# Index cast of the expert choice from ScalarE to VectorE, and another spread of the compression steps, their weight loads and the subtractions beside them

## The chip, the cores and the metric

The kernel runs on one core of a Trainium2 chip. The metric is the device time of one execution in microseconds (us); lower is better. PE is TensorE, DVE is VectorE, ACT is ScalarE, POOL is GpSimd, SP is SyncE. ACT, DVE and POOL each work through one queue in order, so an instruction that waits holds up all that stands behind it on its engine.

## The reference

One decoder layer for 512 tokens of width 1024: a gated linear recurrence (RG-LRU) beside a sparse attention (NSA), merged, then a product-key expert layer (PEER) and a per-layer embedding. Cut to what the change touches:

```python
z_rx, z_rg, z_q, z_kv, z_ng, z_m = split(rmsnorm(h) @ w_in)

# RG-LRU: r, ig are sigmoids of block-diagonal products of xf
log_a = -LRU_C * r * softplus(-lam)
a = exp(log_a)
u = sqrt(-expm1(2.0 * log_a)) * (ig * xf)
hs = scan(a, u)                       # h[t] = a[t] h[t-1] + u[t]
y_a = (hs * gelu(z_rg)) @ w_a

# NSA: 31 blocks of 32 keys (and of 32 values) are compressed by a small MLP
blk = t[:, idx] + pe
hid = gelu(flat(blk) @ w1 + b1)       # w1: 4096 x 256, for keys and for values
kc, vc = hid_k @ w2_k + b2_k, hid_v @ w2_v + b2_v

# PEER: 16 of 16384 experts for each of 8 heads and each token
best, ci = top_k(cand, 16)            # cand: sums of two sorted lists of 16
e_idx = i1[ci // 16] * 128 + i2[ci % 16]
g = softmax(best)
out = sum(gelu(x . u[e_idx]) * g * v[e_idx])
```

## The kernel before, in words

**Products in three parts.** Every float32 product is three PE passes: an operand is cast to fp32r ("hi") and the rest is src - hi ("lo"), and hi·hi, hi·lo and lo·hi are added in PSUM (`mm3`, L131 to L134). `split` (L124 to L129) makes the two: L126 is a cast on ACT, L128 a cast on DVE or POOL, L129 the subtraction (on DVE unless an engine is passed).

**The projections.** The input projection goes through w_in in chunks of 128 columns; a chunk is 24 matmuls of 128x512 (8 k-slices, three passes). `plan` sets the order in which the chunks are loaded by SP, and `look` splits a chunk (`w8_split`, L174) up to three chunks ahead of its product, into a pool of three `w8` buffers. For the chunks of this stage the cast is on DVE (`hi_eng`) and the subtraction on POOL.

**The stage the change spreads anew** (some 90 to 190 us in the profile). After eight `rx` chunks and two `kc` chunks (the compressed keys' input) come ten chunks in the order `seq`: rg0 to rg3, vc0, vc1, rg4 to rg7. "rg" is the gate z_rg (its evacuation is a gelu on ACT, L514), "vc" is the input of the compressed values (its evacuation writes `blk`: L433 adds, L128 casts on DVE, L129 subtracts on POOL). Between k-slices of these chunks, at the places that the table `CSTEP` gives, one step of the generator `compress()` is put on PE: one of 16 "hid" steps for the keys or 16 for the values (four matmuls of 128x256, L478), a copy `hs` (L481), or the transpose `hidT` with its gelu (L485, L488). A hid step needs 256 KB of w1: SP loads it (L446) into one of four buffers (`w1buf`, `w1half`), ACT casts it, DVE subtracts (`w1_split`), two steps ahead of PE (`LAW` is 3).

**The list `side`.** Work of the recurrence is put between chunks by `run_side`: `lru_b(c)` (ACT: tanh and exp; DVE: a square, L406, and L407), `lru_sqrt` (ACT, two of 128x2048, L412), `rot_c` and `rot_d` (sines, L274 to L279), `lru_c(c)` (DVE: a product, L417, and the scan, L418). Sine, square root, exp and gelu need different ACT tables, so ACT loads a table when it goes from one to the other.

**What follows.** `vs` and `vw` are the attention's values: 64 matmuls of 128x256 with the hi weights (L575, L576), then 32 with the lo weights. Then attention, output products, and the expert layer.

**The expert layer.** `choose(i)` is a generator for each of four groups of 128 tokens. It searches on DVE (sorted lists of 8 by MAX8, FIND_INDEX8, MATCH_REPLACE8), casts the found index `bi` to f16 (`ci`, L1161, ACT), folds it into two table positions (L1170 to L1188) and makes the one-hot tables `oh` (L1243, L1244) that the products G (L1220) read. Each `yield n` gives PE about n ns of fill: steps of the product `xu` of 128 rows of the table u with all tokens, whose weights are cast on ACT (`uh`, L1066) and subtracted on DVE (`ul`, L1071), with an evacuation on ACT (`ac`, L1081). Before the cast of `ci`, `choose` puts the next group's scores on PE and four copies of them (L981) on ACT. The gathers of the chosen rows are indirect DMAs from POOL, consumed on DVE (L1272, L1278).

The lines that set the places of the stage before:

```python
seq = [("rg", i) for i in range(4)] + [("vc", 0), ("vc", 1)] + [("rg", i) for i in range(4, 8)]
CSTEP = [(), (), (1, 2, 4, 5, 7), (0, 1, 3, 4, 6, 7), (0, 2, 3, 5, 6, 7), (), (), (1, 2, 4, 5, 7), (0, 1, 3, 4, 6, 7), (0, 2, 3, 5, 6, 7)]
```

Of the kernel before, what the change touches and what calls it, by code (L numbers as in the profile page):

```python
# [94 lines left out]
def tile_hybrid(ctx, tc, a, out, dbg=None):  # L95
# [61 lines left out]
    plan += [chunk("rg", i) for i in range(4)] + [chunk("vc", 0), chunk("vc", 1)]  # L157
    plan += [chunk("rg", i) for i in range(4, 8)]
# [40 lines left out]
    def gemm(jobs, nside=1, nxt=()):  # L199

        keys = [j[:2] for j in jobs] + list(nxt)
        for n, (name, i, mh, ml, evac) in enumerate(jobs):
            look(keys[n:n + 3])
            w = ready.pop((name, i))
            o = bank("z_" + name)
            if key0 == keys[n]:
# [10 lines left out]
            run_side(nside)  # L217
# [84 lines left out]
    y8, e8, s8, q8, t8, ncoef, pcoef = (const.tile([128, 8], F32, name=n)  # L302
                                        for n in ("y8", "e8", "s8", "q8", "t8", "ncoef", "pcoef"))
# [137 lines left out]
    w1n = [0, 0]  # L441

    def w1_load(upto):
        while w1n[0] < min(upto, 32):
            j, l0 = divmod(w1n[0], 16)
            SP.dma_start(w1buf[w1n[0] % 4], a["cmp_w1"][j][:, 2 * l0:2 * l0 + 2].rearrange("p l c -> p (l c)"))  # L446
            w1n[0] += 1

    def w1_split(upto):
        while w1n[1] < min(upto, 32):  # L450
            n = w1n[1]
            split(w1hl[:, n % 4, 0], w1hl[:, n % 4, 1], w1buf[n % 4])
# [6 lines left out]
    gemm([("kc", i, nhi, nlo, ev_kv(0)) for i in range(2)], nside=3, nxt=[("rg", 0), ("rg", 1)])  # L459
# [75 lines left out]
    seq = [("rg", i) for i in range(4)] + [("vc", 0), ("vc", 1)] + [("rg", i) for i in range(4, 8)]  # L535
    CSTEP = [(), (), (1, 2, 4, 5, 7), (0, 1, 3, 4, 6, 7), (0, 2, 3, 5, 6, 7), (), (), (1, 2, 4, 5, 7), (0, 1, 3, 4, 6, 7), (0, 2, 3, 5, 6, 7)]
    for n, key in enumerate(seq):
# [3 lines left out]
        for k in range(KD):  # L541
# [3 lines left out]
            if n > 3 and k in (1, 5):  # L545
                run_side(1)
# [5 lines left out]
        run_side(3 if n == 0 else 0)  # L552
    for _ in comp:
        pass
    hi_eng[0] = None
    hghi = at.tile([128, 8, S], F32R, name="hghi", tag="big0")
    hglo = at.tile([128, 8, S], F32R, name="hglo", tag="big1")
# [574 lines left out]
    def choose(i, order):  # L1132
# [28 lines left out]
        A.copy(ci.rearrange("p (k h) -> p h k", h=NH), bi)  # L1161
# [13 lines left out]
        yield 4250  # L1175
# [400 lines left out]
```

## Time and profile before

| what | value |
|---|---|
| three runs | 1902.70, 1902.98, 1907.99 us, median 1902.98 |
| the profiled execution, its own time | 1904.83 us |
| its span (first to last instruction) | 1902.8 us |
| mean granted TensorE clock | 0.989 of 2.4 GHz |
| busy: PE, DVE, ACT, POOL | 96%, 74%, 44%, 35% of the span |
| chain that ended last, by engine | PE 70%, DVE 17%, issue 3%, ACT 3%, DMA 1% |

PE is busy for 96% of the span, so the time is PE's work and its idle stretches; those are found by asking which instructions PE waited for, and in which window. "Busy" of an engine is the time in its instructions; a table by windows shows it for one stretch, with the share of full clock that TensorE was granted ("PEclk"). A row of a timeline gives start, duration, engine, line, operation, tile out<-in, partitions x elements, and how many alike follow each other; in brackets the idle time before it and what ended that.

### The profile page before, as it was taken

To read this page: it belongs to the slowest core of one execution; us is meant where nothing else is said; L and a number is where in the kernel's file an instruction comes from. 1 tells how busy PE (TensorE), PEld (TensorE's weight loads), DVE (VectorE), ACT (ScalarE), POOL (GpSimd) and SP (SyncE) were. 2 spreads that over 40 slices of the span, in tenths; PEclk is the share of its full clock that TensorE was granted. 3 is DMA by queue.
4 is the path that set the end of the run, shared out by engine and by line. 5 is a ranking of instruction groups with operands and counts; after the bars stand their busy time and mean duration, and the time that the engine had idled before them with its cause. 6 is when DMAs were issued, how large, how long until landed. Compare 5 with 4: busy or idle time off the path is not lost.

```text
span 1902.8 us, 26515 instructions
## 1 busy us (share of the span) xinstructions
PE 1820.9 (96%) x9817; PEld 1592.5 (84%) x9817; DVE 1410.3 (74%) x2642; ACT 834.6 (44%) x1268; POOL 664.6 (35%) x406
## 2 busy tenths in 40 slices
PE   7988999999999999899999999999999999999997
PEld 6767888777779879899899898888888899999986
DVE  6887516666633368998998977888878788888864
ACT  4463323444521434574674663333333333333353
POOL 3443444322135325334335321222222255556400
PEclk9989999999999999999999999999999999999999
DMA  4253232211024525696796998999999899999941
GB/s 170 101 169 114 78 104 74 67 56 45 23 67 166 194 93 193 234 360 245 252 343 240 339 354 311 360 352 354 353 344 353 306 337 338 343 344 344 359 182 45
DMA packets 181858, 433.29 MB, mean 228 GB/s; under 512 B 14560, under 2 KB 88032, under 8 KB 181728
## 3 DMA queue, kind: packets, MB, share of 16 engines
q1 hardware_dynamic: 124272, 250.35, 37.9%
q0 software_dynamic: 37728, 137.38, 19.9%
q10 hardware_dynamic: 19728, 43.86, 6.1%
q8 instruction: 77, 1.26, 0.3%
q14 instruction: 53, 0.43, 0.1%
HBM read 382.25 MB, written 49.28 MB: 227 GB/s over the span
## 4 chain that ended last, share of the span: by engine, by line
PE 70%; DVE 17%; issue 3%; ACT 3%; DMA 1%; POOL 0%; DVEq 0%; ACTq 0%; POOLq 0%
PE va L134 9%; PE va L132 9%; PE va L133 9%; PE xu L134 6%; PE xu L132 6%; PE xu L133 6%; DVE ul L1071 2%; DVE oh L1243 2%; DVE gr L1272 2%; DVE acc L1278 1%; PE G L1220 1%; PE hid L478 1%; PE z_w_a L132 1%; PE z_w_b L133 1%; PE z_w_a L133 1%
## 5 line engine op out<-in xcount | busy, mean ns | idle before, releaser
L134 PE MATMUL xu<-x2hi,ul 128*128 128x384 f32 x1008 | 339.5, 337 | 10.4 <-DVE ul L1071 10.4
L132 PE MATMUL xu<-x2hi,uh 128*128 128x384 f32 x1008 | 343.7, 341 | 2.7 <-ACT ac L1081 2.0
L133 PE MATMUL xu<-x2lo,uh 128*128 128x384 f32 x1008 | 338.3, 336 | 0.0
L132 PE MATMUL va<-v,A 128*128 128x512 f32 x768 | 299.1, 389 | 1.5 <-ACT A L126 1.5
L134 PE MATMUL va<-v,A 128*128 128x512 f32 x768 | 299.2, 390 | 0.0
L133 PE MATMUL va<-v,A 128*128 128x512 f32 x768 | 298.8, 389 | 0.0
L1257 POOL DMA_INDIRECT gr<-in_peer_u,eidx x128 | 167.3, 1307 | 333.1 <-DVE gr L1272 260.4
L1257 POOL DMA_INDIRECT gr<-in_peer_v,eidx x128 | 185.5, 1449 | 278.0 <-DVE acc L1278 218.2
L126 ACT CAST v<-vring 128x1024 fp32r<-128x1024 f32 x128 | 134.7, 1053 | 256.4 <-issue 146.5
L129 DVE TENSOR_TENSOR v<-vring,v 128x1024 fp32r<-128x1024 f32 x128 | 156.5, 1223 | 63.1 <-ACT v L126 63.0
L134 PEld LDWEIGHTS xu<-x2hi,ul 128*128 128x128 f32 x1008 | 190.2, 189 | 12.9 <-DVE ul L1071 12.9
L132 PEld LDWEIGHTS xu<-x2hi,uh 128*128 128x128 f32 x1008 | 190.6, 189 | 5.1 <-ACT ac L1081 2.3
L133 PEld LDWEIGHTS xu<-x2lo,uh 128*128 128x128 f32 x1008 | 190.4, 189 | 1.9
L132 PEld LDWEIGHTS va<-v,A 128*128 128x128 f32 x768 | 144.1, 188 | 30.2 <-ACT A L126 1.8
L134 PEld LDWEIGHTS va<-v,A 128*128 128x128 f32 x768 | 144.1, 188 | 30.2 <-DVE A L129 0.3
L133 PEld LDWEIGHTS va<-v,A 128*128 128x128 f32 x768 | 144.2, 188 | 28.3
L1278 DVE SCALAR_TENSOR_TENSOR acc<-gr,dots,acc 128x1024 f32<-128x1024 f32 x128 | 163.9, 1281 | 2.6 <-DMA gr<-in_peer_v,eidx 1.0
L1272 DVE SCALAR_TENSOR_TENSOR gr<-gr,x2g 128x1024 f32<-128x1024 f32 x128 | 156.8, 1244 | 5.5 <-DMA gr<-in_peer_u,eidx 5.5
L1066 ACT CAST uh<-ur 128x1024 fp32r<-128x1024 f32 x126 | 132.5, 1053 | 61.1 <-ACT ac L1081 31.1
L1081 ACT ACTIVATE ac<-xu 128x384 f32<-128x384 f32 x128 | 64.3, 502 | 181.6 <-PE xu L134 166.8
L1071 DVE TENSOR_TENSOR ul<-ur,uh 128x1024 fp32r<-128x1024 f32 x101 | 124.8, 1242 | 11.4 <-ACT uh L1066 6.0
L1223 ACT ACTIVATE gst<-G 128x512 f32<-128x512 f32 x96 | 100.3, 1155 | 19.8 <-PE G L1220 19.6
(446 smaller groups left out, 3644.6 us busy)
## 6 DMA issues: line engine op xcount, KB each, us to landing
vring<-in_peer_v SPq DMA_DIRECT2D x128, 512.0 KB
ur<-in_peer_uT SPq DMA_DIRECT2D x126, 512.0 KB
gdram<-gst ACTq DMA_DIRECT2D x12, 2048.0 KB
gt<-gdram SPq DMA_DIRECT2D x32, 768.0 KB
xdram<-ac ACTq DMA_DIRECT2D x88, 192.0 KB
vring<-xdram SPq DMA_DIRECT2D x88, 192.0 KB
raw_m<-in_w_in SPq DMA_DIRECT2D x16, 512.0 KB
raw_rx<-in_w_in SPq DMA_DIRECT2D x8, 512.0 KB
```

The lines of the kernel that those rows point to most:

```text
L126: A.copy(hi, src)
L129: (eng or V).tensor_tensor(lo, src, f(hi), op=OP.subtract)
L132: T.matmul(o, sh, mh, start=start, stop=False)
L133: T.matmul(o, sh, ml, start=False, stop=False)
L134: T.matmul(o, sl, mh, start=False, stop=stop)
L1066: A.copy(us[e][0], urs[e])
L1071: (G if search[0] else V).tensor_tensor(us[e][1], urs.pop(e), f(us[e][0]), op=OP.subtract)
L1081: A.activation(ac, o[:, :ND], AF.Gelu_apprx_tanh)
L1223: A.activation(gst[:, :, c:c + 4].rearrange("p a t -> p t a"), o.rearrange("p (t a) -> p t a", t=4), AF.Copy, scale=1.0 / GSC)
L1257: G.indirect_dma_start(out=r, out_offset=None, in_=tab, in_offset=bass.IndirectOffsetOnAxis(ap=eidx[:, j:j + 1], axis=0))
L1272: V.scalar_tensor_tensor(r, r, 1.0, x2g, op0=OP.mult, op1=OP.mult, accum_out=dots[:, j:j + 1])
L1278: V.scalar_tensor_tensor(acc, r, dots[:, j:j + 1], acc, op0=OP.mult, op1=OP.add)
```

## The change

Two parts of the program are touched.

**The choice.** The cast of `bi` to `ci` is put on DVE instead of ACT, in all four groups, and one `yield` has 4700 for 4250, so a little more fill goes ahead of the next step.

**The stage of gates and compression.** The chunk order is rg0 to rg5, vc0, vc1, rg6, rg7. The subtractions of these chunks' weights, of `blk` and of the vs weights are on DVE instead of POOL. The loads of w1 are issued from POOL instead of SP; a step's subtraction comes one step after its cast, and the load that fills its buffer again after that. The square of `lru_b` is a second exp on ACT (coefficient doubled) instead of a DVE product. The hid steps are fewer in each chunk (4, 4, 4, 5, then 4 and 6), and seven of them go into the vs hi product. Square roots, sines and scans go into vc0, vc1, rg6 and rg7 (table `SIDE`), and two `lru_b` each into rg3 and rg4. The split of the small weight `wg`, and `lru_d`, come after the vs hi product.

```diff
-    plan += [chunk("rg", i) for i in range(4)] + [chunk("vc", 0), chunk("vc", 1)]
-    plan += [chunk("rg", i) for i in range(4, 8)]
+    plan += [chunk("rg", i) for i in range(6)] + [chunk("vc", 0), chunk("vc", 1)]
+    plan += [chunk("rg", i) for i in range(6, 8)]
...
-        split(w[:, 0], w[:, 1], r, G, hi_eng[0])
+        split(w[:, 0], w[:, 1], r, lo_eng[0], hi_eng[0])
...
             if c < 8:
+                a2s[c] = t2("a2")
                 A.activation(tt[:, c], rr[:, c], AF.Tanh, scale=pcoef[:, c:c + 1])
+                A.activation(a2s[c], rr[:, c], AF.Exp, scale=n2coef[:, c:c + 1])
                 A.activation(rr[:, c], rr[:, c], AF.Exp, scale=ncoef[:, c:c + 1])
             if c > 0:
-                a2 = t2("a2")
-                V.tensor_tensor(a2, rr[:, c - 1], rr[:, c - 1], op=OP.mult)
-                V.scalar_tensor_tensor(tt[:, c - 1], a2, 1.0, tt[:, c - 1], op0=OP.add, op1=OP.mult)
+                V.scalar_tensor_tensor(tt[:, c - 1], a2s.pop(c - 1), 1.0, tt[:, c - 1], op0=OP.add, op1=OP.mult)
...
-                split(blk[j][:, ab, :, 0, c], blk[j][:, ab, :, 1, c], t, G, V)
+                split(blk[j][:, ab, :, 0, c], blk[j][:, ab, :, 1, c], t, V, V)
...
-            SP.dma_start(w1buf[w1n[0] % 4], a["cmp_w1"][j][:, 2 * l0:2 * l0 + 2].rearrange("p l c -> p (l c)"))
+            G.dma_start(w1buf[w1n[0] % 4], a["cmp_w1"][j][:, 2 * l0:2 * l0 + 2].rearrange("p l c -> p (l c)"))
...
-            split(w1hl[:, n % 4, 0], w1hl[:, n % 4, 1], w1buf[n % 4])
+            A.copy(w1hl[:, n % 4, 0], w1buf[n % 4])
             w1n[1] += 1
+            w1_lo(n)
+        if upto >= 32:
+            w1_lo(32)
+
+    def w1_lo(upto):
+        while w1n[2] < upto:
+            n = w1n[2]
+            V.tensor_tensor(w1hl[:, n % 4, 1], w1buf[n % 4], f(w1hl[:, n % 4, 0]), op=OP.subtract)
+            w1n[2] += 1
             w1_load(n + 5)
...
-    gemm([("kc", i, nhi, nlo, ev_kv(0)) for i in range(2)], nside=3, nxt=[("rg", 0), ("rg", 1)])
+    lo_eng[0] = V
+    gemm([("kc", i, nhi, nlo, ev_kv(0)) for i in range(2)], nside=(2, 1), nxt=[("rg", 0), ("rg", 1)])
...
-    CSTEP = [(), (), (1, 2, 4, 5, 7), (0, 1, 3, 4, 6, 7), (0, 2, 3, 5, 6, 7), (), (), (1, 2, 4, 5, 7), (0, 1, 3, 4, 6, 7), (0, 2, 3, 5, 6, 7)]
+    seq = [("rg", i) for i in range(6)] + [("vc", 0), ("vc", 1)] + [("rg", i) for i in range(6, 8)]
+    CSTEP = [(), (), (1, 3, 5, 7), (1, 3, 5, 7), (1, 3, 5, 7), (0, 2, 3, 5, 7), (), (), (4, 5, 6, 7), (0, 1, 3, 4, 6, 7)]
+    SIDE = [(5,), (), (), (0, 0), (0, 0), (1,), (0, 0, 4), (0, 3, 6), (1, 2, 5), (1, 4, 6)]
...
+                if br == 0 and k % 4 == 3:
+                    next(comp, None)
...
-        A.copy(ci.rearrange("p (k h) -> p h k", h=NH), bi)
+        V.tensor_copy(ci.rearrange("p (k h) -> p h k", h=NH), bi)
...
-        yield 4250
+        yield 4700
```

What the order of the instructions makes of it, at three places. First DVE's queue around chunks rg2 and rg3 (w is a chunk's weights, w1hl a step's w1, tt and a or a2 the recurrence's), before:

```order
L407 SCALAR_TENSOR_TENSOR tt<-a_779,tt 128x512
L129 TENSOR_TENSOR wgl<-wg,wgh 128x192
L129 TENSOR_TENSOR w1hl<-w1buf,w1hl 128x512
L128 CAST w_798<-raw_rg 128x1024
L406 TENSOR_TENSOR a_829<-rr 128x512
L407 SCALAR_TENSOR_TENSOR tt<-a_829,tt 128x512
```

and with the change:

```order
L128 CAST w_850<-raw_rg 128x1024
L129 TENSOR_TENSOR w_850<-raw_rg,w_850 128x1024
L464 TENSOR_TENSOR w1hl<-w1buf,w1hl 128x512 x2
L464 TENSOR_TENSOR w1hl<-w1half,w1hl 128x512 x2
L464 TENSOR_TENSOR w1hl<-w1buf,w1hl 128x512
L128 CAST w_915<-raw_rg 128x1024
L129 TENSOR_TENSOR w_915<-raw_rg,w_915 128x1024
L410 SCALAR_TENSOR_TENSOR tt<-a_805,tt 128x512
L410 SCALAR_TENSOR_TENSOR tt<-a_922,tt 128x512
L464 TENSOR_TENSOR w1hl<-w1buf,w1hl 128x512
```

Each chunk's subtraction now stands in DVE's queue behind its cast, ahead of the w1 subtractions of that chunk's steps, and the squares (L406) are gone from it.

Second ACT's queue around chunks rg2 to rg4, with the change (before, these tanh and exp stood ahead of the chunks' steps, in the kc chunks and in rg0):

```order
L527 ACTIVATE gr<-z_rg 128x512
L406 ACTIVATE tt<-rr,pcoef 128x512
L407 ACT_TABLE_LOAD
L407 ACTIVATE a_922<-rr,n2coef 128x512
L408 ACTIVATE rr<-rr,ncoef 128x512
L406 ACTIVATE tt<-rr,pcoef 128x512
L407 ACTIVATE a_927<-rr,n2coef 128x512
L408 ACTIVATE rr<-rr,ncoef 128x512
L455 CAST w1hl<-w1half 128x512 x2
L455 CAST w1hl<-w1buf 128x512 x2
L527 ACT_TABLE_LOAD
```

Two `lru_b` with their six activations and two table loads now stand among the four w1 casts of rg3, and the same again in rg4.

Third DVE's queue at the end of a search, group i=1, before:

```order
L1164 TENSOR_TENSOR g<-bv 128x8x16
L1170 TENSOR_TENSOR wk<-thr,ci 128x1024
L1171 TENSOR_SCALAR cx<-ci 128x128
L1172 TENSOR_TENSOR wk<-wk,lens 128x1024
L1173 TENSOR_TENSOR ci<-ci,cx 128x128
```

and with the change:

```order
L1177 CAST ci<-bi 128x8x16
L1180 TENSOR_TENSOR g<-bv 128x8x16
L1186 TENSOR_TENSOR wk<-thr,ci 128x1024
L1187 TENSOR_SCALAR cx<-ci 128x128
L1188 TENSOR_TENSOR wk<-wk,lens 128x1024
```

The comparison that reads `ci` (L1170 before, L1186 with the change) has its input from DVE itself.

## Rows read from the trace of the kernel before

**Rows 1.** Busy time by windows of the stage: PE, PEld, DVE, ACT, POOL, PEclk, DMA.
```profile
105.00:120.00 15.00, 10.54 (x34) 8.11 (x35) 14.11 (x13) 1.87 (x4) 8.02 (x3) 0.66 0.52 172
140.00:160.00 20.00, 14.89 (x72) 12.26 (x70) 19.51 (x19) 6.34 (x11) 13.41 (x7) 0.99 0.30 99
160.00:180.00 20.00, 19.94 (x105) 17.31 (x106) 16.90 (x23) 8.88 (x14) 3.54 (x2) 0.92 0.50 158
```

**Rows 2.** What PE waited for, 90 to 200 us: total, times, longest.
```profile
PE hid L478 <- DVE w1hl L129: 8.0, 2, 5.2
PE z_rg L132 <- DVE w L128: 3.0, 1, 3.0
PE z_rg L134 <- POOL w L129: 1.8, 2, 1.5
```

**Rows 3.** Timeline of PE, 151 to 162 us: start, duration, instruction.
```profile
151.58 0.63 PE L478 MATMUL hid<-w1hl,blk 128*124 128x256 f32 x4
152.05 0.39 PE L132 MATMUL z_rg<-nhi,w 128*128 128x512 f32 x1
152.28 0.40 PE L133 MATMUL z_rg<-nlo,w 128*128 128x512 f32 x1
...
160.86 0.63 PE L132 MATMUL z_rg<-nhi,w 128*128 128x512 f32 x1
161.28 0.63 PE L133 MATMUL z_rg<-nlo,w 128*128 128x512 f32 x1
```

**Rows 4.** Timeline of DVE, 101 to 155 us.
```profile
101.47 0.69 DVE L407 SCALAR_TENSOR_TENSOR tt<-a,tt 128x512 f32<-128x512 f32 x1
...
104.28 0.69 DVE L128 CAST w<-raw_rg 128x1024 fp32r<-128x1024 f32 x1
...
105.61 2.72 DVE L407 SCALAR_TENSOR_TENSOR tt<-a,tt 128x512 f32<-128x512 f32 x1
...
153.74 1.22 DVE L418 TENSOR_TENSOR_SCAN rr<-rr,gx 128x512 f32<-128x512 f32 x1
```

**Rows 5.** Timeline of POOL at 105 us.
```profile
105.20 2.58 POOL L129 TENSOR_TENSOR w<-raw_rg,w 128x1024 fp32r<-128x1024 f32 x1 [4.92 <-DVE w L128]
```

**Rows 6.** Groups by line and form on DVE, 90 to 186 us: busy, mean ns.
```profile
L129 DVE TENSOR_TENSOR w1hl<-w1half,w1hl 128x512 fp32r<-128x512 f32 x16 | 15.9, 1015 | 6.1 <-ACT w1hl L126 6.1
...
L418 DVE TENSOR_TENSOR_SCAN rr<-rr,gx 128x512 f32<-128x512 f32 x8 | 13.9, 1735 | 0.3
...
L128 DVE CAST blk<-blkt 128x496 fp32r<-128x496 f32 x7 | 7.9, 1124 | 0.2
```

**Rows 7.** The same subtraction of 128x1024 on DVE, later in the kernel.
```profile
L129 DVE TENSOR_TENSOR v<-vring,v 128x1024 fp32r<-128x1024 f32 x128 | 156.5, 1223 | 63.1 <-ACT v L126 63.0
```

**Rows 8.** Groups by line and form on ACT, 90 to 186 us.
```profile
L403 ACT ACTIVATE rr<-rr,ncoef 128x512 f32<-128x512 f32 x7 | 5.1, 725 | 0.2
...
L403 ACT ACT_TABLE_LOAD x1 | 1.3, 1283 | 0.0
```

**Rows 9.** A w1 load from SP's queue, and the cast that waited for it.
```profile
117.74 0.93 SPq L446 DMA_DIRECT2D w1half<-in_cmp_w  x2
...
120.54 0.62 ACT L126 CAST w1hl<-w1half 128x512 fp32r<-128x512 f32 x1 [0.86 <-DMA w1half<-in_cmp_w]
```

**Rows 10.** Four loads from POOL's queue, and the instruction that waited for the first.
```profile
1816.87 2.13 POOL L1453 DMA_DIRECT2D h<-hdram  x4
...
1825.46 1.29 DVE L1365 TENSOR_TENSOR h<-acc,h 128x512 f32<-128x512 f32 x2 [5.97 <-DMA h<-hdram]
```

**Rows 11.** What DVE waited for, 700 to 1160 us: total, times, longest.
```profile
DVE wk L1170 <- ACT ci L1161: 19.2, 4, 8.2
```

**Rows 12.** What PE waited for, 905 to 1060 us (groups i=1 and i=2 of the choice).
```profile
PE G L1220 <- DVE oh L1244: 7.0, 7, 3.3
PE xu L134 <- DVE ul L1071: 3.7, 3, 2.1
```

More of the change, by code (lines that the diff above doesn't have):

```diff
@@ L170, in tile_hybrid @@
     ready = {}
-    hi_eng = [None]
+    hi_eng, lo_eng = [None], [G]
     def w8_split(n, key):
@@ L216, in gemm @@
                 post.append(r)
-            run_side(nside)
+            run_side(nside[n] if isinstance(nside, tuple) else nside)
     cst = const.tile([128, C_N], F32, name="cst")
@@ L299, in to_T @@
             split(hi[:, c, ts], lo[:, c, ts], o.rearrange("p (j t) -> p j t", j=4))
-    y8, e8, s8, q8, t8, ncoef, pcoef = (const.tile([128, 8], F32, name=n)
-                                        for n in ("y8", "e8", "s8", "q8", "t8", "ncoef", "pcoef"))
+    y8, e8, s8, q8, t8, ncoef, pcoef, n2coef = (const.tile([128, 8], F32, name=n)
+                                        for n in ("y8", "e8", "s8", "q8", "t8", "ncoef", "pcoef", "n2coef"))
     def coef_a():
@@ L327, in coef_d @@
         V.tensor_scalar(pcoef, y8, 8.0, None, op0=OP.mult)
+        V.tensor_scalar(n2coef, y8, -16.0, None, op0=OP.mult)
     def first(i):
@@ L397, in tile_hybrid @@
     gemm([("rx", i, nhi, nlo, ev_rx) for i in range(8)], nxt=[("kc", 0), ("kc", 1)])
+    a2s = {}
     def lru_b(c):
@@ L440, in tile_hybrid @@
     w1buf = [p.tile([128, 512], F32, name="w1buf", tag="qn") for _ in range(2)] + [w1half[:, 0], w1half[:, 1]]
-    w1n = [0, 0]
+    w1n = [0, 0, 0]
     def w1_load(upto):
@@ L519, in tile_hybrid @@
     wgl = p.tile([128, KD, 24], F32R, name="wgl", bufs=1)
-    split(wgh, wgl, wg)
     comp = compress()
-    side += [lru_sqrt(0), lru_sqrt(4), rot_c, rot_d] + [lru_c(c) for c in range(8)]
+    side += [lru_sqrt(0), lru_sqrt(4)] + [lru_c(c) for c in range(3)] + [rot_c, rot_d] + [lru_c(c) for c in range(3, 8)]
     def pair_split(n, which, j, tiles):
@@ L527, in pair_split @@
         c = slice(j * 128, (j + 1) * 128)
-        split(tiles[0][:, :, c], tiles[1][:, :, c], r, G)
+        split(tiles[0][:, :, c], tiles[1][:, :, c], r, lo_eng[0])
     def pair(n):
@@ L534, in tile_hybrid @@
     w1_split(1)
-    seq = [("rg", i) for i in range(4)] + [("vc", 0), ("vc", 1)] + [("rg", i) for i in range(4, 8)]
-    CSTEP = [(), (), (1, 2, 4, 5, 7), (0, 1, 3, 4, 6, 7), (0, 2, 3, 5, 6, 7), (), (), (1, 2, 4, 5, 7), (0, 1, 3, 4, 6, 7), (0, 2, 3, 5, 6, 7)]
+    seq = [("rg", i) for i in range(6)] + [("vc", 0), ("vc", 1)] + [("rg", i) for i in range(6, 8)]
+    CSTEP = [(), (), (1, 3, 5, 7), (1, 3, 5, 7), (1, 3, 5, 7), (0, 2, 3, 5, 7), (), (), (4, 5, 6, 7), (0, 1, 3, 4, 6, 7)]
+    SIDE = [(5,), (), (), (0, 0), (0, 0), (1,), (0, 0, 4), (0, 3, 6), (1, 2, 5), (1, 4, 6)]
     for n, key in enumerate(seq):
@@ L544, in tile_hybrid @@
                 next(comp, None)
-            if n > 3 and k in (1, 5):
-                run_side(1)
+            run_side(SIDE[n].count(k))
             if n == 9 and k == 3:
@@ L551, in tile_hybrid @@
         (ev_rg if key[0] == "rg" else ev_kv(1))(key[1], o)
[L552 to L557, printed above, removed]
+    hi_eng[0], lo_eng[0] = None, G
+    hg = []
     def lru_d(c):
@@ L561, in go @@
             V.tensor_tensor(gr[:, c], rr[:, c], gr[:, c], op=OP.mult)
-            split(hghi[:, c], hglo[:, c], gr[:, c])
+            split(hg[0][:, c], hg[1][:, c], gr[:, c])
         return go
-    side += [lru_d(c) for c in range(8)]
     vv = at.tile([128, 2, NT, 2, 256], F32R, name="vv", tag="vv")
@@ L576, in tile_hybrid @@
                 T.matmul(os[i][:, :256], nlo[:, k, ts], hl[0][:, k], start=False, stop=False)
+                if br == 0 and k % 4 == 3:
+                    next(comp, None)
         if br == 0:
+            for _ in comp:
+                pass
+            hghi = at.tile([128, 8, S], F32R, name="hghi", tag="big0")
+            hglo = at.tile([128, 8, S], F32R, name="hglo", tag="big1")
+            hg += [hghi, hglo]
+            side += [lru_d(c) for c in range(8)]
+            split(wgh, wgl, wg)
             hls[1] = pair("vw")
```

## The prediction

> **What bounds the kernel now.** I read the page's busy shares first: PE works for nearly the whole span, so the kernel gets faster only where PE idles or runs at the low clock, and I then asked for PE's waits by window. Two places touch the change.
>
> The first is the stage of gates and compression. Between 90 and 200 us PE waits 8.0 us in hid steps for a w1 subtraction, 3.0 us for a chunk's cast and 1.8 us for a chunk's subtraction on POOL [rows 2]: 12.8 us, nearly all in two windows, 105 to 120 and 140 to 160, where DVE is busy for 14.1 of 15 and 19.5 of 20 us [rows 1]. Behind the waits the granted clock falls, to 0.66 on the mean of 105 to 120 and to 0.92 in 160 to 180 [rows 1]; the reader sees the level in the spacing of matmuls of 512 columns, 0.23 us (152.05 to 152.28) at 2.4 GHz and 0.42 us (160.86 to 161.28) right after a wait, at 1.2 GHz [rows 3]. A mean of 0.66 over 15 us is 10.2 us at the lower level; PE was busy for 70% of them, and half of that is lost: 3.6 us. For 160 to 180 the same working gives 3.2 us at the lower level and 1.6 us lost. So the stage holds 12.8 + 5.2 = **18.0 us** that a better order could win at most. From there to attention PE hardly waits, so what the stage wins moves the rest forward.
>
> The second is the choice. DVE waits four times for the cast of `ci` on ACT, 19.2 us in all, 8.2 us at the longest [rows 11]. That cast stands behind four score copies and an evacuation paced by PE. Two of the waits are of 8.2 us (groups 1 and 2); the other two share under 3 us. In the same two groups PE waits 7.0 us for one-hot tables and 3.7 us for `ul`, all from DVE [rows 12].
>
> **The change part by part.**
>
> *Subtractions from POOL to DVE.* Ten chunks and the two halves of vs at 1.22 us [rows 7] are 14.6 us more on DVE, and eight of `blk` at about 0.69 us, the price of a 512-wide two-input instruction [rows 4], are 5.5 us more. The eight squares that go to ACT give back 8 x 0.69 = 5.5. Against the 14.6 us: while POOL subtracts, DVE's instructions stretch. L407 takes 0.69 us alone and 2.72 us when it starts 0.4 us after a POOL subtraction of 2.58 us [rows 4, 5]. Sixteen w1 subtractions took 1015 ns on the mean (some 690 alone), eight scans 1735 ns (1.22 us alone), seven casts of `blk` 1124 ns (about 420 where POOL was quiet is not in the rows; 0.69 as a bound) [rows 4, 6]: 5.2 + 4.1 + 3.0 = 12.3 us of stretching in these three groups alone, and others stretch too. DVE's total thus comes out between even and some 10 us less. The long one begins with POOL's, so I take the stretching as POOL's doing, and as gone with it. PE's 1.8 us for POOL's own lateness go as well.
>
> *Steps spread.* Before, five or six hid steps are packed into a chunk; now four (rg2 to rg4), so a chunk lasts 24 x 0.23 + 4 x 0.47 = 7.4 us on PE [rows 3]. DVE needs in it 0.69 + 1.22 + 4 x 0.69 + about two L410 at 0.69 = 6.0 us [rows 4, 7]. That fits, if the queue's order allows it.
>
> *Where the new waits are.* I bound them twice. By totals from below: in rg3 and rg4 ACT has six tanh or exp at 0.725, two table loads at 1.28 [rows 8], four w1 casts at 0.62 [rows 9] and a gelu of some 0.7: 10.1 us against PE's 7.4, so 2.7 us too much in each, 5.4 us together, of which the two-step lead of the casts (2 x 1.85 us) hides up to 3.7: at least 1.7 us late. From vc0 to the end of the vs hi product DVE has two chunks (3.8), vs (2.4), four pieces of `blk` at three instructions (up to 8.3), eight `lru_c` at 0.69 + 1.22 (15.3) and seventeen w1 subtractions (11.7): 41.5 us; PE has 4 x 5.5 + 17 x 0.47 + 64 x 0.115 = 37.4 us. So 4.1 us of waiting there, since no part of it can move out. Together 5.8 us at least. By order from above: at some eight places (rg4 to rg7 and the steps in vs) a w1 subtraction stands behind a cast, a subtraction and one or two instructions of the recurrence that themselves wait for ACT or for a `w8` buffer: 0.69 + 1.22 = 1.9 us each [rows 4, 7], 15.3 us. I take 12, nearer the upper end, because a queue in order can't use its idle stretches for later chunks. Each single wait stays below the 3.0 and 5.2 us after which the clock fell, so I take none of the clock's 5.2 us back. **Stage: 18.0 - 12 = 6 us won**, between 18.0 - 15.3 = 2.7 and 18.0 - 5.8 = 12.2.
>
> *w1 loads from POOL.* A load took 2.8 us from SP's issue to the cast that waited for it [rows 9]. From POOL's queue the trace has only larger ones in a crowd: four issues in 2.13 us (0.53 each), the first landed 8.6 us after its issue [rows 10]. Bounds: 2.8 to 8.6 us; I take 3.5, since these loads are half as big as those and POOL has nothing else to do here. A buffer comes round every four steps, 7.4 us; load, cast and subtraction take 3.5 + 0.62 + 0.69 = 4.8. Hidden; the point from which they decide is a load of 6.1 us. The Trainium skill's DMA: Bandwidth & Descriptors, section Issuing engine by pattern, sends plain loads to Sync, and its estimate for a load from GpSimd is 2.0 us plus bytes by 436 GB/s, 2.6 us for these; by that the sum stays as it is.
>
> *Second exp, more tables.* Eight exp (5.8 us) and two more table loads (2.6 us) [rows 8] lie on ACT; they are counted in rg3 and rg4 above. `wg` and `lru_d` come later, beside the vs lo product, where ACT and DVE have room; I cost them at nothing. If their cover failed, it would be some 1 us.
>
> *The choice.* With the cast on DVE, right behind the search, the two long waits go. The cast itself has an eighth of the elements of a 1.22 us instruction [rows 7]: between 0.15 and 1.22 us, four times; I take 0.4, as it reads an odd layout. DVE comes 7.8 us earlier, but then meets the next instruction that waits: an `ul` whose cast on ACT goes at PE's pace. So in group 1 only some 4 of its waits go, in group 2 nearly all of 5. The two other groups have little to gain (under 3 us of waiting in rows 11, and the first gathered rows are late next). PE's ten waits of 10.7 us [rows 12] shrink by **9 us**, between 3 (only the first wait of each group) and 10.7. The 450 ns of additional fill per group move work, they add none.
>
> **Sum.** 6 + 9 = 15 us. The profiled execution took 1904.83 us, 1.9 us above the median of the runs shown; on it the sum gives 1889.8, on the median 1903.0 it gives **1888.0**.
>
> **The rivals.**
>
> 1. *The stage comes out near its bound.* If the queues interleave as the totals allow, the stage wins 12.2 us and the choice 10.7: 1903 - 23 = 1880. For it: DVE is freed of the stretching. Against: 4.1 us of DVE's surplus in the values cannot be hidden. With a somewhat lower DVE surplus the time reaches 1877.
> 2. *ACT and DVE are the bound of the stage again.* Waits of 15.3 us come in bunches (rg4 to rg6, and the end of vs), the clock falls in two places as before (5.2 us): 18.0 - 20.5 = -2.5, and the choice +9: 1896.5. For it: before, three waits of 3.0, 1.5 and 2.8 us within ten brought the clock down, and such bunches are what the new order makes.
> 3. *The choice gives nothing back.* DVE's time is won, but the gathers or the next `ul` end last: +0 to +3 there, and the stage +6: 1894 to 1897. Against: the waits of rows 12 name DVE, and in these windows PE waits for no DMA.
> 4. *Loads of w1 come late: slower.* The subtractions of DVE hold up POOL while it writes the loads' descriptors, or the loads take as long as those of rows 10. With 10 us for a load a round of four steps lasts 10 + 1.3 = 11.3 instead of 7.4 us, 1.0 us per step, 28 us over 28 steps: 1888 + 28 = 1916. The point at which the change loses is a load of 8.1 us, where 0.5 us per step eat the 15 us. The section SWDGE vs HWDGE vs iDMA of the Trainium skill's DMA: Bandwidth & Descriptors says that DVE in its two-port mode locks GpSimd out of the rings that it writes; no run here shows it on loads yet.
> 5. *The subtractions stretch on DVE for another cause* (the DMA share in 105 to 120 is 0.52 [rows 1]), so nothing is won from POOL's silence and DVE carries 14.6 us more: that would be about 1900. Rows 4 and 5 speak against it, as the long L407 begins with POOL's subtraction.
>
> **How the numbers follow.** Forecast, 1882 to 1896: 0.56. Rival 1: 0.14. Rival 2: 0.12, rival 3: 0.06, rival 5: 0.04, rival 4: 0.08. No change means within 0.3% (5.7 us), about what a measurement of this kernel can tell. Faster by more (below 1897.3) are the forecast, rival 1, half of rival 2 and half of rival 3: 0.79. Within are the other halves and rival 5: 0.13. Slower is rival 4: 0.08. The range of 1877 to 1901 takes in rivals 1 to 3 and 5; it leaves out rival 4 and the edges.
>
> **What would show it.** Right: L421 (the scan) near 1.22 us and w1 subtractions near 0.69 us on the mean, no POOL row among PE's waits, PE's waits in the stage at 9 to 13 us, each under 3 us, with a clock near 1.0 throughout, and the start of the vs lo product 6 us earlier; no DVE wait for `ci`, PE's waits for `oh` and `ul` in groups 1 and 2 under 2 us. Wrong: ACT's w1 casts waiting for their DMA for many us (rival 4), waits over 3 us with a granted clock of 0.5 behind them (rival 2), or DVE's waits in the choice moved to gathered rows or `uh` (rival 3).

## The result, and the profile after

The changed kernel takes 1896.81 us (median of seven runs, 1892.98 to 1899.06), the kernel before on the same chip 1906.13 us (seven runs, 1902.70 to 1909.65). The ratio is 0.9945, with a 95% interval from 0.993 to 0.9961: faster by 0.4 to 0.7%. The forecast was 1888.0 us, 15 us less than the 1903.0 us that three runs of before had shown; 9 to 10 us came, from the 1906.13 us of seven runs.

The page of the changed kernel's profiled execution (1896.81 us), head and busy shares; PE's work is the same, the span 7.8 us shorter:

```profile
span 1895.0 us, 26509 instructions
...
PE 1819.3 (96%) x9817; PEld 1594.3 (84%) x9817; DVE 1401.5 (74%) x2658; ACT 840.3 (44%) x1274; POOL 648.8 (34%) x419
```

To see where the time went, I cut both profiled executions at the same instructions, by their starts in PE's timeline: the first gate product, the first vs lo product, the first fill product `xu`, the last group of G, the first `va` (the product of the chosen experts with v, behind the last group of the choice). First of before (189.41 - 90.55 = 98.9 us for the stage):

```profile
90.55 0.39 PE L132 MATMUL z_rg<-nhi,w 128*128 128x512 f32 x1
...
189.41 0.40 PE L586 MATMUL v<-w8vsl,nhi 128*128 128x256 f32 x2
...
690.95 0.53 PE L132 MATMUL xu<-x2hi,uhl 128*128 128x384 f32 x1
...
1124.66 1.07 PE L1220 MATMUL G<-oh 128*128 128x128 f16 x16
...
1150.88 0.50 PE L132 MATMUL va<-v,A 128*128 128x512 f32 x1 [1.49 <-ACT A L126]
```

and of the changed kernel (184.79 - 90.52 = 94.3):

```profile
90.52 0.39 PE L132 MATMUL z_rg<-nhi,w 128*128 128x512 f32 x1
...
184.79 0.49 PE L602 MATMUL v<-w8vsl,nhi 128*128 128x256 f32 x2
...
685.66 0.52 PE L132 MATMUL xu<-x2hi,uhl 128*128 128x384 f32 x1
...
1113.98 1.07 PE L1236 MATMUL G<-oh 128*128 128x128 f16 x16
...
1143.48 0.50 PE L132 MATMUL va<-v,A 128*128 128x512 f32 x1 [1.49 <-ACT A L126]
```

The same cuts for every kernel of this study, in us (one profiled execution each, so a row says less than a ratio over many runs). "The end" is the start of PE's last matmul, some 10 us before the span's end:

| kernel | stage | to the first xu | choice, to the last G | last G to va | va to the end |
|---|---|---|---|---|---|
| before | 98.9 | 501.5 | 433.7 | 26.2 | 741.5 |
| the change | 94.3 | 500.9 | 428.3 | 29.5 | 741.1 |
| e1_choice | 99.3 | 501.5 | 427.4 | 29.0 | 739.9 |
| e2_cast | 99.2 | 501.6 | 426.1 | 27.0 | 748.2 |
| e3_stage | 94.9 | 500.6 | 434.4 | 26.2 | 741.0 |
| e4_v_later | 95.8 | 496.9 | 427.8 | 24.9 | 741.8 |
| e5_sp_loads | 92.9 | 498.5 | 427.0 | 30.4 | 740.4 |
| e6_lo_pool | 104.1 | 499.8 | 428.4 | 29.3 | 739.1 |
| e7_lo_dve | 95.4 | 503.6 | 433.4 | 25.8 | 741.5 |
| f1_v_later_4250 | 95.1 | 498.5 | 425.4 | 25.5 | 739.9 |
| g1_all | 92.9 | 496.9 | 426.6 | 25.5 | 741.5 |
| g2_scans_later | 92.0 | 501.0 | 425.4 | 25.5 | 738.9 |
| g3_square_dve | 99.5 | 498.4 | 423.2 | 28.9 | 740.9 |
| g4_before_v_later | 103.5 | 498.8 | 433.7 | 25.5 | 738.8 |

The stage gave 4.6 us and the choice 5.4 us up to the last G; right behind it 3.3 us were lost. The stage's difference holds over several executions: with its code of before it took 98.9, 99.3, 99.2 and 103.5 us, with the change's 94.3, 94.9, 95.8 and 95.1. In five executions (e6, e7, f1, g2, g4) the granted clock was 0.91 already between 60 and 80 us, and the stage began 1 to 3 us later than in the others. The last column holds nothing that the change touches and still differs by some us from one execution to the next. The second column holds what the change put behind the vs hi product (`wg` and `lru_d`); it takes 501.4 us on the mean of the five executions with the old places (e7 among them) and 499.1 on the nine with the new ones. No run here tells whether the change does that.

**The stage after.** What PE waited for, 90 to 200 us; these answer to [rows 2]:

```profile
PE hid L491 <- DVE w1hl L464: 9.4, 9, 3.0
PE hid L491 <- DVE blk L129: 1.2, 1, 1.2
```

10.6 us for 12.8: the waits for POOL and for the chunk's cast are gone, and nine waits for w1, one of them of 3.0 us, stand for two long ones. The windows that answer to [rows 1]:

```profile
105.00:120.00 15.00, 13.74 (x72) 11.16 (x71) 7.89 (x12) 10.37 (x15) 4.30 (x8) 1.00 0.58 192
...
140.00:160.00 20.00, 15.73 (x72) 12.75 (x71) 18.34 (x26) 9.56 (x12) 0.54 (x1) 0.90 0.18 60
160.00:180.00 20.00, 17.99 (x109) 15.51 (x109) 16.40 (x22) 9.44 (x15) 5.38 (x10) 0.93 0.61 197
```

From 105 to 120 us PE is busy for 13.74 instead of 10.54 us, at a granted clock of 1.00 instead of 0.66. But in 140 to 180 the clock falls again, behind the longest wait. PE's timeline there, to be read like [rows 3]:

```profile
155.23 0.28 PE L491 MATMUL hid<-w1hl,blk 128*124 128x256 f32 x1
158.55 1.00 PE L491 MATMUL hid<-w1hl,blk 128*124 128x256 f32 x3 [3.04 <-DVE w1hl L464]
159.35 0.63 PE L132 MATMUL z_rg<-nhi,w 128*128 128x512 f32 x1
159.78 0.63 PE L133 MATMUL z_rg<-nlo,w 128*128 128x512 f32 x1
```

The matmuls of 512 columns are 0.43 us apart (1.2 GHz). DVE's timeline shows why PE waited: the w1 subtraction stands behind six instructions on `blk` (the last is the first row here), the sine, a product and a scan.

```profile
154.98 0.68 DVE L129 TENSOR_TENSOR blk<-blkt,blk 128x496 fp32r<-128x496 f32 x1
155.57 0.48 DVE L279 TENSOR_SCALAR sinT<-sinT,cst 128x512 f32<-128x512 f32 x1
155.97 0.68 DVE L420 TENSOR_TENSOR gx<-gx,tt 128x512 f32<-128x512 f32 x1
156.69 1.23 DVE L421 TENSOR_TENSOR_SCAN rr<-rr,gx 128x512 f32<-128x512 f32 x1
157.83 0.67 DVE L464 TENSOR_TENSOR w1hl<-w1buf,w1hl 128x512 fp32r<-128x512 f32 x1
```

DVE's instructions no longer stretch (groups by form, to [rows 6]; scans from 1735 to 1225 ns, w1 subtractions from 1015 to 685):

```profile
L464 DVE TENSOR_TENSOR w1hl<-w1half,w1hl 128x512 fp32r<-128x512 f32 x16 | 10.5, 685 | 4.6 <-ACT w1hl L455 4.5
L421 DVE TENSOR_TENSOR_SCAN rr<-rr,gx 128x512 f32<-128x512 f32 x8 | 9.8, 1225 | 0.3
```

**The choice after.** In the answer that had [rows 11], DVE's waits of 700 to 1160 us, no wait for `ci` is left (the cast itself takes 0.45 us on DVE, once 1.17); at its head stand now:

```profile
DVE v L129 <- ACT v L126: 15.8, 4, 12.9
DVE ul L1087 <- PE xu L134: 8.3, 2, 4.6
```

PE's waits in groups 1 and 2 (896 to 1051 us, the same instructions as in [rows 12]) are one line of 4.1 us, for 10.7 before:

```profile
PE G L1236 <- DVE oh L1260: 4.1, 3, 2.0
```

Over the whole way from the first `xu` to the last G, PE idles 433.71 - 410.15 = 23.6 us before and 428.32 - 412.29 = 16.0 us with the change, 7.5 us less. Of these, 2.1 us are taken up by the additional fill (PE is busy 2.1 us longer), which leaves the 5.4 us of the table:

```profile
690.95:1124.66 433.71, 410.15 (x2792) 396.03 (x2790) 403.22 (x1078) 265.40 (x349) 164.83 (x91) 0.98 0.77 278
...
685.66:1113.98 428.32, 412.29 (x2803) 399.01 (x2802) 405.85 (x1081) 262.71 (x345) 171.84 (x92) 0.98 0.79 282
```

DVE's wait of 12.9 us is at the end. ACT's timeline behind the last G:

```profile
1116.77 0.41 ACTq L1242 DMA_DIRECT2D gdram<-gst  x1
...
1120.19 1.05 ACT L1082 CAST uh<-ur 128x1024 fp32r<-128x1024 f32 x1 [0.40 <-ACT ac L1097]
1128.65 1.04 ACT L126 CAST v<-vring 128x1024 fp32r<-128x1024 f32 x1 [7.40 <-DMA gdram<-gst]
1129.60 0.48 ACT L1097 ACTIVATE ac<-xu 128x384 f32<-128x384 f32 x1
```

The first `v` is cast into room that `gst` held until its last store of 2 MB is out: 11.9 us from issue to cast. ACT waits for it 7.40 us, with the evacuation `ac` behind it in its queue, for which PE then waits. Before, the same cast waited 3.6 us and hurt PE hardly. PE's waits of 1100 to 1145 us in the changed kernel:

```profile
PE xu L132 <- ACT ac L1097: 2.5, 1, 2.5
PE va L132 <- ACT A L126: 1.5, 1, 1.5
PE xu L134 <- DVE ul L1087: 1.4, 1, 1.4
```

The windows from the last G to `va`, before and after, show what this costs. PE idles 5.4 us instead of 1.9, and the granted clock is 0.94 instead of 1.00; although twelve products fewer (2.1 us) stand there, the stretch is 3.3 us longer:

```profile
1124.66:1150.88 26.22, 24.31 (x149) 23.67 (x148) 8.37 (x9) 11.76 (x17) 1.61 (x1) 1.00 0.86 312
...
1113.98:1143.48 29.50, 24.08 (x137) 23.12 (x136) 9.24 (x10) 11.71 (x16) 1.68 (x1) 0.94 0.82 285
```

### The profile page after: what moved, and what is told of

Same layout as the page of the kernel before. It is cut to its first block, busy times and chain, and to the rows that moved or that the text cites. A ratio compares the mean times of both kernels' runs of the same rounds, so it can differ in the third digit from the quotient of the medians.

```text
span 1895.0 us, 26509 instructions
## 1 busy us (share of the span) xinstructions
PE 1819.3 (96%) x9817; PEld 1594.3 (84%) x9817; DVE 1401.5 (74%) x2658; ACT 840.3 (44%) x1274; POOL 648.8 (34%) x419
## 4 chain that ended last, share of the span: by engine, by line
PE 73%; DVE 16%; ACT 4%; issue 4%; DMA 3%; POOL 0%; SPq 0%; DVEq 0%; ACTq 0%; POOLq 0%
PE va L132 9%; PE va L134 9%; PE va L133 9%; PE xu L134 7%; PE xu L132 7%; PE xu L133 7%; DVE ul L1087 2%; DVE oh L1259 2%; DVE gr L1288 1%; PE G L1236 1%; PE z_m L132 1%; PE z_m L133 1%; PE z_m L134 1%; DVE acc L1294 1%; PE sc L996 1%
## 5 line engine op out<-in xcount | busy, mean ns | idle before, releaser
L134 PEld LDWEIGHTS va<-v,A 128*128 128x128 f32 x768 | 144.1, 188 | 30.4 <-DVE A L129 0.3
L1239 ACT ACTIVATE gst<-G 128x512 f32<-128x512 f32 x96 | 100.4, 1160 | 13.9 <-PE G L1236 13.6
```

Source lines behind the costliest of these rows:

```text
L134: T.matmul(o, sl, mh, start=False, stop=stop)
L1239: A.activation(gst[:, :, c:c + 4].rearrange("p a t -> p t a"), o.rearrange("p (t a) -> p t a", t=4), AF.Copy, scale=1.0 / GSC)
```

## The experiments

Each ratio is to the kernel before on the same chip, with its 95% interval; between the experiments the chip changed (one for e1 to e4, one for e5 to f1, one for g1 to g4), so two of them are compared by their ratios. Stages and gaps are in the table above.

**e1_choice: the choice alone.** On the kernel before:

```diff
-        A.copy(ci.rearrange("p (k h) -> p h k", h=NH), bi)
+        V.tensor_copy(ci.rearrange("p (k h) -> p h k", h=NH), bi)
...
-        yield 4250
+        yield 4700
```

> The kernel before with both edits of the choice (cast of ci on DVE, 4700 for 4250), nothing of the stage. Theory: the choice wins about 5.4 us up to the last product G and gives 3.3 us back right behind it, where ACT's queue waits for the last store of G with fewer steps of fill left to cover it; so 2 us faster than before (ratio 0.999). Rival: the choice's gain is kept when the stage is left alone: 5 to 9 us faster (0.995 to 0.997).

0.9988 (0.9972 to 1.0005). Up to the last G 6.3 us less than before, behind it 2.8 us more: as the theory said, with 3.5 us left in the profile; over the runs it can't be told from no change.

**e2_cast: the cast without the additional fill.** The first of the two edits.

> The kernel before with the cast of ci on DVE alone, the fill left at 4250. Theory: the additional fill of 450 ns per group is what takes the cover away from the store behind the last G; without it the give-back is smaller (under 1.5 us) and PE's waits for G in groups 1 and 2 are a little longer: 3 to 5 us faster than before. Rival: the give-back comes from the earlier start alone, since the store lasts as long as DMA traffic makes it; then this is as fast as with 4700, within 1 us.

0.997 (0.9956 to 0.9983), 5.5 us by the medians. Behind the last G only 0.8 us is lost, and ACT's wait for the store is 4.4 us instead of 7.2 us in e1_choice:

```profile
ACT v L126 <- DMA gdram<-gst: 4.4, 1, 4.4
```

So by the profiles the give-back hangs on the fill; over the runs the intervals of e1 and e2 overlap. PE's waits in groups 1 and 2 are as long as with 4700 (5.4 us, e1 5.3), so the additional fill bought nothing there. Its cost can be counted: in the trace of the changed kernel 120 products `xu` remain behind the last G, as in e1, before the change 132, as here; the twelve take 2.1 us at the 0.18 us that they stand apart. They were spent as fill in the groups, and are missing where the store needs cover. (The profiled execution of this kernel took 6.7 us more in its va loop, 3.8 us of it in longer waits for `uh` and `ul`, whose rows of u came late; the median doesn't show it.)

**e3_stage: the stage alone.** The changed kernel with both edits of the choice undone.

> The changed kernel with the choice as before (cast on ACT, 4250). Theory: the stage keeps its 4.5 us (vs lo product at 184.8 instead of 189.4), and nothing in the choice: 4.5 us faster than before (0.9976). Rival: what the stage wins is eaten by later waits: within 1 us of before.

0.997 (0.9954 to 0.9985), 5.6 us by the medians. The stage is 94.9 us, the choice as before (434.4 and 26.2). By the point values the stage is the larger part of the total; the intervals of e1 and e3 overlap.

**e4_v_later: the first v one fill step later.** On the changed kernel:

```diff
-        if nst[0] == nst0 + 2 and 0 not in vs:
+        if nst[0] == nst0 + 3 and 0 not in vs:
```

> The changed kernel with the first v split one fill step later behind the last G (third instead of second of five). Theory: ACT's queue then reaches the cast that waits for the last store of G one step (4.2 us) later, so PE's waits of 2.5 us for ac and 1.4 us for ul there go, and the low clock behind them: 3 to 5 us faster than the changed kernel, 12 to 14 us faster than before (0.993). Rival: the wait only moves to the start of the va loop, for want of v: no gain.

0.9928 (0.9913 to 0.9944), 1891.25 us. From the last G to va 24.9 instead of 29.5 us, and PE waits no longer for `ac`:

```profile
PE va L132 <- ACT A L126: 1.5, 1, 1.5
PE xu L134 <- DVE ul L1087: 1.2, 1, 1.2
```

The wait did not move to the va loop: ACT still waits 4.3 us for the store, but PE is no longer held up by it, and the clock there is 1.00. This shows the store's wait as the place where the choice's gain went. (Over the runs the interval overlaps that of the change; f1, g1 and g2, with the same edit, take 25.5 us there.)

**e5_sp_loads: w1 from SP again.**

```diff
-            G.dma_start(w1buf[w1n[0] % 4], a["cmp_w1"][j][:, 2 * l0:2 * l0 + 2].rearrange("p l c -> p (l c)"))
+            SP.dma_start(w1buf[w1n[0] % 4], a["cmp_w1"][j][:, 2 * l0:2 * l0 + 2].rearrange("p l c -> p (l c)"))
```

> The changed kernel with the 32 loads of w1 issued from SP again. Theory: loads from POOL land some 0.5 to 1.5 us later than from SP (3.0 to 4.4 us to the waiting cast, against 2.8), and PE hardly feels it; the vs lo product starts within 1 us of the changed kernel's 184.8 us, and the time is within 3 us of it. Rival: the late loads are what PE's waits in the stage come from (ACT waits 14.7 us for them): the start at 182 us or earlier and PE's waits under 8 us.

0.9937 (0.9911 to 0.9964): over the runs not to be told from the change. The vs lo product starts at 183.67 us, 1.1 us earlier, about what the theory allowed and far from the rival's 182. In the profile the stage is 92.9 us, 1.4 less than with loads from POOL, and PE waits 9.0 us instead of 10.6; g1_all, with loads from SP too, has 92.9 again, the four kernels with this stage and loads from POOL 94.3 to 95.8. The loads from POOL are thus a small loss within the change, not its bound. ACT's waits for w1 loads stay at 14.0 us (14.7 with POOL), so nearly all of them come with the new order and not with POOL.

**e6_lo_pool: the subtractions on POOL again.**

```diff
-    lo_eng[0] = V
+    lo_eng[0] = G
...
-                split(blk[j][:, ab, :, 0, c], blk[j][:, ab, :, 1, c], t, V, V)
+                split(blk[j][:, ab, :, 0, c], blk[j][:, ab, :, 1, c], t, G, V)
```

> The changed kernel with the subtractions of chunks, blk and vs on POOL again, ahead of the w1 loads in POOL's queue. Theory: POOL's subtractions stretch DVE's instructions as before (scans above 1.6 us on the mean, w1 subtractions above 0.85) and hold up the loads in the queue, so the stage loses all that the change won and more: vs lo product at 187 to 195 us, 2 to 10 us slower than the changed kernel. Rival: the spread of the steps alone makes the gain; the start stays within 1 us of 184.8.

0.9977 (0.996 to 0.9993). Over the runs the gain of the stage is mostly gone. In the profile the stage takes 104.1 us, 9 to 10 more than with the change (95.1 in f1, whose clock was low ahead of the stage too). Whether it is worse than before isn't shown: the code of before took 98.9 to 103.5 us, the latter in such an execution (g4), and the ratio is below 1. DVE stretches again (groups by form on DVE; the 13 subtractions from `w1half` stay at 681 ns), and ACT waits 18.5 us for w1buf loads that stand behind subtractions in POOL's queue:

```profile
L464 DVE TENSOR_TENSOR w1hl<-w1buf,w1hl 128x512 fp32r<-128x512 f32 x14 | 15.9, 1140 | 3.9 <-ACT w1hl L455 3.9
L421 DVE TENSOR_TENSOR_SCAN rr<-rr,gx 128x512 f32<-128x512 f32 x8 | 14.0, 1747 | 0.3
```

and in the list of waits:

```profile
ACT w1hl L455 <- DMA w1buf<-in_cmp_w: 18.5, 8, 9.6
```

Both causes, the stretching and the late loads, work here at once; this run doesn't part them. The Trainium skill says in the GPSIMD Engine Reference, section 8 (Key points), that GpSimd shares its SBUF interfaces with VectorE; the trace agrees (scans of 1747 ns with POOL subtracting, 1225 without).

**e7_lo_dve: only the subtractions to DVE.** On the kernel before, the engine of these subtractions, nothing else.

> The kernel before with those subtractions on DVE, and nothing else of the change. Theory: the stretching goes (scans at 1.22 us, w1 subtractions at 0.69), but five or six steps to a chunk leave DVE no room for 20 us more, so the stage gains nothing: vs lo product at 187 to 193 us (189.4 before). Rival: the stretching was the whole loss; start at 185 us or earlier, as with the full change.

0.9989 (0.9973 to 1.0004). The vs lo product starts at 187.56 us, inside the theory's 187 to 193, but from a stage that began 1.6 us later; the stage itself is 95.4 us, 3.5 less than before, without any spread, where the theory said that it gains nothing. Scans are at 1224 ns. The places are still too tight (from 105 to 120 the clock is 0.77 and PE busy for 8.19 of 15 us):

```profile
105.00:120.00 15.00, 8.19 (x34) 6.48 (x35) 12.64 (x18) 4.09 (x8) 0.00 (x0) 0.77 0.63 200
```

Over the runs it can't be told from no change, so that the 3.5 us rest on one execution. How much of the stage's gain the moved subtractions make, and how much the spread adds, thus stays open.

**f1_v_later_4250: later split, and fill at 4250.** The edit of e4_v_later, and `yield 4250` again.

> The changed kernel with the first v split one fill step later and the fill at 4250 again. Theory: both keep steps of fill behind the last G, and one of them is enough; the time is within 2 us of the one with the later split alone (ratio 0.9928 to before). Rival: they add up, as the cast alone with 4250 won 3.4 us over 4700 in the kernel before: 0.991 or less.

0.992 (0.9897 to 0.9943), against 0.9928: they don't add, or by less than these runs tell. In this trace ACT's cast no longer waits for the store at all.

**g1_all: later split, 4250, w1 from SP.** The edits of f1_v_later_4250 and e5_sp_loads together.

> The changed kernel with three edits: first v split one step later, fill at 4250, w1 loads from SP. Theory: the parts add, since each takes a wait at another place: the stage (first gate product to vs lo product) 92.9 us as with SP loads alone, the way from the last G to the va loop 24 to 25 us; 15 to 18 us faster than before, ratio 0.991. Rival: a later wait takes them back; no faster than the one with the later split alone (0.9928).

0.9884 (0.9863 to 0.9906), 1884.97 us: 20 us faster than before by the medians and 12 us faster than the change. It is more than its parts in the profile promise: stage 6.0, choice 7.1 and the way to va 0.7 make 13.8 us; 4.6 us stem from the second column, which these three edits don't touch. By its median it is the fastest kernel of the study; g2_scans_later can't be told from it.

**g2_scans_later: two scans behind the steps of rg6.** On g1_all:

```diff
-    SIDE = [(5,), (), (), (0, 0), (0, 0), (1,), (0, 0, 4), (0, 3, 6), (1, 2, 5), (1, 4, 6)]
+    SIDE = [(5,), (), (), (0, 0), (0, 0), (1,), (0, 0, 4), (0, 3, 6), (1, 6, 7), (1, 4, 6)]
```

> The same three edits, and two scans of chunk rg6 put behind its last but one step instead of in front of its steps. Theory: PE's wait of 3.0 us in rg6 is a w1 subtraction behind a scan in DVE's queue; with the scan behind it the wait falls to about 1 us, the clock does not fall there, and the stage takes 91 to 92 us (92.9 with SP loads). Rival: DVE's work in these chunks is the bound, the wait only moves into rg7 and the vs product: 92.9 us or more.

0.9895 (0.9875 to 0.9915). The wait of 3.0 us is 1.2 us, as said, and the stage 92.0 us for 92.9. The waits are more and shorter (10.0 us in twelve, 8.9 in nine before it):

```profile
PE hid L491 <- DVE w1hl L464: 8.8, 11, 1.2
PE hid L491 <- DVE blk L129: 1.2, 1, 1.2
```

and the windows, where g1_all had a clock of 0.94 and 0.89:

```profile
140.00:160.00 20.00, 17.41 (x83) 13.90 (x81) 17.82 (x26) 10.72 (x13) 0.00 (x0) 1.00 0.19 59
160.00:180.00 20.00, 16.18 (x107) 14.16 (x108) 17.03 (x23) 9.25 (x14) 0.00 (x0) 1.00 0.62 199
```

So DVE's surplus stays, spread finer, and what is won is the clock. In the total nothing shows.

**g3_square_dve: the squares as DVE products.** On the changed kernel:

```diff
-                A.activation(a2s[c], rr[:, c], AF.Exp, scale=n2coef[:, c:c + 1])
...
+                V.tensor_tensor(a2s[c - 1], rr[:, c - 1], rr[:, c - 1], op=OP.mult)
```

> The changed kernel with the squares as DVE products again, not as a second exp. Theory: in rg3 and rg4 ACT has too much to do (10.1 us to PE's 7.4), so eight exp less (0.72 us each, four of them in rg3 and rg4) win about 1.5 us of PE's waits there, and eight DVE products more cost about as much later: stage 93 to 95 us (94.3). Rival: DVE's queue is the tighter one everywhere: 96 us or more.

0.9963 (0.9947 to 0.9979). My theory was wrong, the rival right in the profile: the stage takes 99.5 us, 3.7 to 5.2 more than in the four executions with the change's stage (over the runs the interval overlaps that of the change). PE waits 14.3 us, three times for about 3 us, and the clock is 0.91 in 120 to 140 and 0.83 in 160 to 180:

```profile
PE hid L491 <- DVE w1hl L464: 13.1, 7, 3.1
```

and the two windows:

```profile
120.00:140.00 20.00, 16.60 (x82) 13.68 (x80) 12.62 (x18) 12.05 (x17) 4.26 (x8) 0.91 0.49 161
...
160.00:180.00 20.00, 14.83 (x69) 12.53 (x70) 18.12 (x25) 7.24 (x11) 4.68 (x9) 0.83 0.49 157
```

By the traces it is DVE's own work that makes the difference, not a wait for ACT: the product waits 1.6 us for ACT's exp here, and in the changed kernel L410 waits 2.1 us for the second one. But until rg2 three products of 0.69 us stand in DVE's queue that the changed kernel lacks, and the first w1 subtraction of rg2 starts at 105.12 us instead of 103.47; first here, then in the changed kernel:

```profile
105.12 1.28 DVE L464 TENSOR_TENSOR w1hl<-w1buf,w1hl 128x512 fp32r<-128x512 f32 x2
...
103.47 1.29 DVE L464 TENSOR_TENSOR w1hl<-w1buf,w1hl 128x512 fp32r<-128x512 f32 x2
```

Without the second exp the stage is no shorter in the profile than before (98.9).

**g4_before_v_later: the later split on the kernel before.** The edit of e4_v_later on the kernel before.

> The kernel before with the first v split one fill step later and nothing else. Theory: before the change the fill behind the last G covers the store, ACT's wait for it held nobody up but ul for 0.4 us, so at most 1 us is won from the last G to the va loop (25.4 us): ratio 0.999 to 1.001. Rival: the later split is an improvement of its own, as large as behind the change: 24 us or less there, and 4 us in the total.

0.999 (0.9971 to 1.0009), and 25.5 instead of 26.2 us to va. So by itself the later split gives 0.7 us in the profile; more than that it is worth only behind the change. (This execution had its stage at 103.5 us, with the clock lower than usual already ahead of it; the code there is that of before.)

## Why the prediction came out as it did

**Direction and range held; the size was too large by some 5 us.** 1896.81 us lies in the range (1877 to 1901), just outside the forecast's own 1882 to 1896. Of the 8.8 us by which it missed 1888.0, 3.1 are the base: before took 1903.0 us in the three runs shown, 1906.1 in seven.

**The stage: right, 4.6 for 6 us.** Its terms came close. Waits that I took as 12 us were 10.6, but not all at the places that I had counted: 4.3 us of them came in rg2 to rg4, so in the total there is some luck. POOL's part went, the stretching went with it (e7 moves the subtractions alone and the scans are at 1224 ns; e6 moves them back and they are at 1747). The term that failed is "I take none of the clock's 5.2 us back": a wait of 3.04 us came, hardly longer than the 3.0 us that I had named as the limit, and the clock was 0.90 and 0.93 in two windows. By the working of the prediction these are 4.0 us at the lower level, PE busy for 79% and half of that lost, 1.6 us, and 2.8 us at 90%, 1.3 us: 2.9 us. 18.0 - 10.6 - 2.9 = 4.5, which is what the cuts give. That it fits to 0.1 us is luck: read off the timeline, the matmuls from 158.55 to 163.0 lose about 2.2 us, not 2.9. g2, which puts two scans behind the steps, shows that the wait came from the scans in DVE's queue.

**w1 loads from POOL: mis-sized.** I took 3.5 us and hid them. The trace has 3.0 to 4.4 us from POOL's issue to the cast that waited (104.45 to 108.84 the longest that I read), and the stage is 1.4 to 2.9 us longer than with loads from SP (e5, g1), single executions all. ACT waited 14.7 us for w1 loads instead of 6.7, but that comes with the new order and not with POOL, since it is 14.0 us with SP's loads (e5). The Trainium skill's estimate in DMA: Bandwidth & Descriptors, section Anatomy of one DMA — SWDGE (gpsimd) path, 2.6 us, was too low for these; its advice in the section Issuing engine by pattern to send plain loads by Sync held in the profiles, for one to three us. Rival 4 stayed far off, since 8.1 us would have been needed.

**The second exp: my account of rg3 and rg4 was wrong.** I had counted ACT's eight exp as a burden there. g3 shows the other way round: with DVE products in their place the stage is 3.7 to 5.2 us longer. `wg` and `lru_d`, which I cost at nothing, have no run of their own; the second column is no longer with them than without.

**The choice: the mechanism right, the step on the fill wrong.** All four waits for `ci` went, 19.2 us. PE's waits in groups 1 and 2 fell from 10.7 to 4.1, by 6.6 us and not by the 9 that I had forecast; over the whole choice PE idled 7.5 us less. So that size was too large. The step that failed is the sentence "The 450 ns of additional fill per group move work, they add none." Moved work has to be missing somewhere: twelve `xu` products ran ahead of the last G and no longer covered its store, ACT's queue stood 7.4 us in front of `ac`, and there PE idled 3.5 us more and lost 1.9 us to the lower clock (e1, e2, e4). I had read [rows 12] up to the last G and not asked what the fill behind it hid. So 9 us became 7.5 - 3.5 - 1.9 = 2.1, which is the table's 5.4 - 3.3. With the store's wait out of the way (f1) the table gives 8.3 + 0.7 = 9.0 us. That this is the size forecast is luck: the 0.7 us come from the later split alone (g4), and of the 8.3 only 5.8 are idle time of PE, the rest a granted clock of 0.99 for 0.98 over that stretch.

**The rivals.** Rival 3 (the choice gives nothing back) came nearest, 1894 to 1897, but by another cause than the gathers: a store's room. DVE's one wait for gathered rows grew from 5.5 to 8.2 us, and no wait of PE names them. Rival 2 was half right (the clock did fall, once, behind a wait of 3.04 us that followed one of 1.23). Rival 5 is refuted by e7's scans at 1224 ns.

## What to carry to other kernels

Fill that is given to one gap is taken from another: before enlarging it, find what the last of it covered, and above all an instruction in an in-order queue that waits for a DMA. Moving that one instruction a step later won 4.6 us here in the profile. Where a second engine's instructions share time with the bound engine, look at the same instruction's duration with and without the neighbour before counting busy shares.

## What the runs showed of the hardware

- One wait of PE of 3.04 us was followed by matmuls at 1.2 GHz for some 4.5 us (158.55 to 163.0); where it was 1.2 us long, in g2, the granted clock stayed at 1.00.
- A store of 2 MB from ACT's queue, with gathers and loads running beside it, held its room for 11.9 us (1116.77 to 1128.65) from its issue; before, for 10.3 us (1127.38 to 1137.63).
- The w1 subtraction of 128x512 on DVE took 685 ns on the mean in the stage where POOL subtracts nothing, and 1015 ns (from `w1half`) in the stage of before, where POOL does; the scan 1225 and 1735 ns.
- The va loop and the end, which no edit touched, differed between executions by 9 us (738.8 to 748.2), and the stage with the code of before by 4.6 us (98.9 to 103.5), so that single executions tell less than their cuts seem to.
